# Norms: one over the root by token in columns, and eight layer norms with their means on TensorE

## The chip, the cores and the metric

The kernel runs on one core of a Trainium2 chip. The metric is the time of one execution on the device in microseconds (us). The engines: TensorE (PE; PEld is its weight load), VectorE (DVE), ScalarE (ACT), GpSimd (POOL) and SyncE (SP), which issues nearly all DMAs. Each engine works through its own instructions in the order in which they were placed, and waits for the others by semaphores.

## The reference

Two transformer blocks over 256 tokens with 1024 channels. The first has four branches (a softmax attention with forget gates, a recurrent unit, a stick-breaking attention, an attention to a memory), each gated, and a feed-forward part. The second has two layers over two streams (context and latent), each with a mixer (attention, gated linear attention, a convolution of width 31) and a feed-forward part. What this change touches are the norms:

```python
def _rms(x, g):
    y = x32 * lax.rsqrt(jnp.mean(x32 * x32, axis=-1, keepdims=True) + EPS)
    return y * g

def _layernorm(x, g=None, b=None):
    xc = xf - jnp.mean(xf, -1, keepdims=True)
    y = xc * lax.rsqrt(jnp.mean(xc * xc, -1, keepdims=True) + NORM_EPS)
    ...

def _modulate(x, shift, scale):
    return _layernorm(x) * (1.0 + scale) + shift

def _post(x, f, gate, g, b):
    return _layernorm(ALPHA * x + gate * f, g, b)
```

Every norm is over channels, so one number per token (or per token and head): the heads' norms of q and k in three attentions, of the linear attention's output, and the layer norms before and after each part.

## The kernel before

Activations lie with channels on the partitions: a stream is `[128, 8, 256]`, eight tiles of 128 channels by 256 tokens. Weights stream from HBM in units of 128x1024 (L438 to 470): a raw unit is split by ScalarE into a high part (`whi`) and by VectorE or GpSimd into a low part (`wlo`), and each product is three passes of 256 columns in a faster format (`mm<-hh,whi`, `hl,whi`, `hh,wlo`). In layer 1 some units go in plain fp32 (`mm<-h,raw`).

A sum over channels is a sum over partitions, and TensorE makes it: a product of a matrix of ones with the squares (L576 to 594, L807, L898, L1115, L1262) leaves the sum of each token in all 128 partitions, as 256 or 512 columns in the one PSUM buffer `st`. One over the root follows on VectorE in eight instructions (`rsqrt`, L530: a scale, a first guess from the bits, twice three instructions of Newton's step; tiles `nv`, `nr`, `nt`) over the same 256 or 512 columns. Its result multiplies the tiles directly, since it is in every partition.

Only two users have the sums in another shape: `token_rsqrt` (L542) lets the squares be the stationary operand and one column of ones the moving one, so the sums come out with tokens on the partitions, two or four columns in all, and the eight instructions are over 2 or 4 columns. The attentions that scale their logits by row use it.

A layer norm (`ln_core`, L603) has two forms. In the slow form VectorE adds the eight tiles (`fsum`, one reduction of 2048 elements), TensorE sums over partitions, VectorE centres all 2048 columns at once, ScalarE squares, VectorE adds the squares (`sq`), one product sums them, and `rsqrt` follows. In the fast form TensorE sums the eight tiles (eight products of 256 columns), VectorE centres two tiles at a time, TensorE sums the eight squares, ScalarE takes a square root and VectorE its reciprocal (`root`, L557). Thirteen of sixteen calls are slow.

A scheduler places the instructions by its own costs. Norms are written as generators that are interleaved with other parts (`weave`, `step`), so most norms have products of another part between their steps on TensorE.

Of the kernel before, what the change touches and what calls it, by code (L numbers as in the profile page):

```python
# [18 lines left out]
P = 128  # L19
D = 1024  # L20
T = 256
KT = 8
# [250 lines left out]
def run(*gens):  # L273
    for g in gens:
        for _ in g:
            pass
# [45 lines left out]
class Builder:  # L322
# [219 lines left out]
    def token_rsqrt(self, sq, nd, n):  # L542
# [9 lines left out]
        return self.rsqrt(ps[:, :2 * nh], 2 * nh, n)  # L552

# [22 lines left out]
    def total_sq(self, x, fast):  # L576
        ps = self.st()[:, :T]
        sq = []
        for f in range(0, KT, 2):
            a = self.t("sq", 512)  # L580
            self.act(a, flat(x[:, f:f + 2]), AF.Square)
            if fast:
                for j in range(2):
                    self.mm(ps, self.ones(), a[:, j * T:(j + 1) * T], start=f + j == 0, stop=f + j == KT - 1)
            else:
                sq.append(a)
                if f % 4:
                    self.tt(sq[-2], sq[-2], a, ALU.add)
# [5 lines left out]
        return ps  # L594

    def rms_h(self, x, g, hh, hl, fast=False):
        r = self.root(self.total_sq(x, fast), T, D)
# [5 lines left out]
    def ln_core(self, x, xc, fast=False):  # L603
# [6 lines left out]
        if fast:  # L610
            return self.root(self.total_sq(xc, True), T, D)
        return self.rsqrt(self.total_sq(xc, False), T, D)
# [55 lines left out]
    def block1(self, xt, ct, fill):  # L668
        nc = self.nc
        with self.pool("b1") as bp, self.phase("b1t", t1=4, t2=6):  # L670
# [7 lines left out]
            nc.sync.dma_start(self.pv[:, :late], self.a["pv"][:, :late])  # L678
            mh = newy()
# [52 lines left out]
            self.rms_h(xt, "ffn_g", *h, True)  # L732
# [74 lines left out]
    def mem_norm(self, ps, out, g):  # L807
# [4 lines left out]
        st = self.st()  # L812
        for j in range(2):
            self.mm(st[:, :T], self.ones(), sq[:, j * T:(j + 1) * T], start=j == 0, stop=j == 1)
        r = self.rsqrt(st[:, :T], T, 256)
# [60 lines left out]
    def fox(self, h, y, bp):  # L876
# [21 lines left out]
        def norm(ps, tag, g):  # L898
# [4 lines left out]
            self.mm(st, self.cst("b64"), sq)  # L903
            r = self.rsqrt(st, 512, 64)
# [210 lines left out]
    def qk_norm(self, ps, out, g):  # L1115
# [4 lines left out]
        st = self.st()  # L1120
        self.mm(st, self.ones(), sq)
        self.stt(out, raw, g, self.rsqrt(st, 512, 128), ALU.mult, ALU.mult)
# [72 lines left out]
    def gla_pair(self, l, hp, qk, vg, glr, S, new_S):  # L1195
# [50 lines left out]
        st = self.st()  # L1246
        for i in range(2):
# [14 lines left out]
            for dv in range(2):  # L1262
# [375 lines left out]
```

## Time and profile before

| | us |
|---|---|
| runs of the kernel | 3063.51 median (3053.55, 3063.51, 3064.5) |
| profiled execution, its own time | 3057.49 |
| its span in the profile | 3055.3 |
| PE busy | 2805.1 (92%) |
| DVE busy | 2004.4 (66%) |
| ACT busy | 1408.2 (46%) |
| POOL busy | 923.8 (30%) |
| granted PE clock, mean | 0.971 |

The span is cut into the parts of the program in order: block 1 with its four branches to about 850 us (its forget-gate attention from 240 to 430), the mixer of the context from 850 to 1400, that of the latent stream to 1850, two feed-forward parts to 2260, the memory and the mixer of layer 1 to 2845, a last feed-forward part. A row of a view gives busy time and the idle time in front of the instructions with what ended it; idle time of PE is the one that matters most, as it is the busiest engine.

### The profile page before, as it was taken

The page shows a single profiled execution, that of the slowest core. Times are in us where ns is not written, and L with a number is a line of the kernel's source. Part 1 is how long each engine was busy: PE and PEld are TensorE (multiplying, and loading weights), DVE is VectorE, ACT ScalarE, POOL GpSimd, SP SyncE. Part 2 cuts the span into 40 slices and gives each one's busy share as a digit, 9 for nine tenths or more (in the row PEclk, how much of TensorE's full clock was granted, in tenths as well). Part 3 has the DMA queues.
Part 4 walks back from the last instruction along what each step waited for, and adds up shares of the span by engine and source line. Part 5 has one row for each costly group of instructions (what it writes and reads, how often), then busy time and mean ns, then how long its engine had stood idle before and what let it go on. Part 6 is the DMA issues. An engine that isn't in the chain of part 4 may idle for free.

```text
span 3055.3 us, 51829 instructions
## 1 busy us (share of the span) xinstructions
PE 2805.1 (92%) x20816; PEld 2626.8 (86%) x20816; DVE 2004.4 (66%) x3305; ACT 1408.2 (46%) x2127; POOL 923.8 (30%) x684
## 2 busy tenths in 40 slices
PE   7998889999998878799999999999999999998898
PEld 6897778888898778788899988998898788898898
DVE  7597763347855999956798344467344499674554
ACT  5464456544445434345645554445434332354443
POOL 3243322233324444641102104444320113453000
PEclk9999999999999989899999999999999999999999
DMA  5443334566456554688567986654643223344353
GB/s 196 146 159 130 125 112 177 179 250 246 154 203 237 193 211 173 238 304 287 210 233 249 330 307 254 239 188 172 250 147 119 97 97 124 118 161 144 126 180 109
DMA packets 153425, 578.32 MB, mean 189 GB/s; under 512 B 17628, under 2 KB 17756, under 8 KB 146656
## 3 DMA queue, kind: packets, MB, share of 16 engines
q1 hardware_dynamic: 152496, 574.45, 53.2%
q8 instruction: 163, 2.67, 0.3%
q14 instruction: 78, 0.64, 0.1%
q10 hardware_dynamic: 688, 0.56, 0.1%
HBM read 516.73 MB, written 58.20 MB: 188 GB/s over the span
## 4 chain that ended last, share of the span: by engine, by line
PE 46%; DVE 19%; ACT 4%; DMA 2%; issue 1%; POOL 1%; SPq 0%; DVEq 0%; ACTq 0%; POOLq 0%
PE mm L371 38%; DVE ca L364 7%; PE st L371 2%; DVE gF L361 2%; DMA raw<-in_ws 2%; PE av L371 1%; DVE sq L361 1%; PE ga L371 1%; DVE wlo L361 1%; PE ad L371 1%; POOL wlo L361 1%; DVE fsum L572 1%; ACT whi L358 1%; PE ov L371 1%; PE lg L371 1%
## 5 line engine op out<-in xcount | busy, mean ns | idle before, releaser
L358 ACT ACTIVATE whi<-raw 128x1024 fp32r<-128x1024 f32 (+1 forms) x706 | 735.9, 1045 | 838.5 <-PE mm L371 529.3
L361 POOL TENSOR_TENSOR wlo<-raw,whi 128x1024 fp32r<-128x1024 f32 (+1 forms) x282 | 717.1, 2545 | 1046.1 <-ACT whi L358 825.6
L361 DVE TENSOR_TENSOR wlo<-raw,whi 128x1024 fp32r<-128x1024 f32 (+1 forms) x315 | 397.7, 1263 | 356.9 <-ACT whi L358 345.8
L371 PE MATMUL mm<-hh,whi 128*128 128x256 f32 x3376 | 504.6, 291 | 18.9 <-ACT hh L358 5.5
L371 PE MATMUL mm<-hh,wlo 128*128 128x256 f32 x3376 | 495.7, 288 | 15.2 <-DVE wlo L361 10.1
L371 PE MATMUL mm<-hl,whi 128*128 128x256 f32 x3376 | 493.0, 288 | 0.0
L371 PEld LDWEIGHTS mm<-hh,whi 128*128 128x128 f32 x3376 | 448.9, 196 | 43.7 <-issue 9.0
L371 PEld LDWEIGHTS mm<-hh,wlo 128*128 128x128 f32 x3376 | 448.4, 196 | 18.5 <-DVE wlo L361 10.5
L371 PEld LDWEIGHTS mm<-hl,whi 128*128 128x128 f32 x3376 | 446.9, 195 | 3.8 <-issue 3.1
L364 DVE SCALAR_TENSOR_TENSOR ca<-yp,pv,ca 128x256 f32<-128x256 f32 x720 | 360.9, 556 | 2.0
L371 PE MATMUL mm<-yh,whi 128*128 128x256 f32 x1152 | 174.6, 291 | 14.6 <-ACT yh L358 10.1
L371 PE MATMUL mm<-h,raw 128*128 128x256 f32 x800 | 181.9, 381 | 0.0
L361 POOL TENSOR_TENSOR gF<-cum 128x128 f32<-128x128 f32 x192 | 99.8, 550 | 255.0 <-PE ga L371 142.0
L371 PEld LDWEIGHTS mm<-yh,whi 128*128 128x128 f32 x1152 | 154.6, 195 | 21.2 <-ACT yh L358 13.2
L371 PE MATMUL mm<-yh,wlo 128*128 128x256 f32 x1152 | 168.1, 288 | 4.9 <-DVE wlo L361 3.9
L371 PE MATMUL mm<-yl,whi 128*128 128x256 f32 x1152 | 168.7, 288 | 2.6 <-DVE yl L364 2.6
L371 PEld LDWEIGHTS mm<-h,raw 128*128 128x128 f32 x800 | 150.3, 191 | 19.3
L371 PEld LDWEIGHTS mm<-yh,wlo 128*128 128x128 f32 x1152 | 152.4, 196 | 6.8 <-DVE wlo L361 4.1
L371 PEld LDWEIGHTS mm<-yl,whi 128*128 128x128 f32 x1152 | 152.9, 195 | 3.3 <-DVE yl L364 2.8
L371 PE MATMUL mm<-hidh,whi 128*128 128x256 f32 x704 | 102.9, 287 | 0.5 <-ACT hidh L358 0.5
L371 PE MATMUL mm<-hidl,whi 128*128 128x256 f32 x704 | 102.2, 286 | 0.0
L371 PE MATMUL mm<-hidh,wlo 128*128 128x256 f32 x704 | 101.5, 285 | 0.0
(280 smaller groups left out, 3840.6 us busy)
## 6 DMA issues: line engine op xcount, KB each, us to landing
raw<-in_ws SPq DMA_DIRECT2D x744, 512.0 KB, 3.8
lo<-wlo SPq DMA_DIRECT2D x109, 512.0 KB, 3.0
wlo<-lo SPq DMA_DIRECT2D x109, 512.0 KB, 4.2
wada<-in_wa SPq DMA_DIRECT2D x48, 1024.0 KB, 5.9
raw<-in_ws SPq DMA_DIRECT2D x32, 384.0 KB, 3.0
memt<-in_tok SPq DMA_DIRECT2D x4, 256.0 KB, 4.7
xt<-in_tok SPq DMA_DIRECT2D x1, 1024.0 KB, 7.1
ct<-in_tok SPq DMA_DIRECT2D x1, 1024.0 KB
```

The costliest lines, as they stand in the source:

```text
L358: return self.nc.scalar.activation(out, in_, f, **k)
L361: return (eng or self.nc.vector).tensor_tensor(out=out, in0=a, in1=b, op=op)
L364: return self.nc.vector.scalar_tensor_tensor(out=out, in0=a, scalar=s, in1=b, op0=op0, op1=op1)
L371: return self.nc.tensor.matmul(out, lhsT=l, rhs=r, start=start, stop=stop, **k)
L572: self.nc.vector.tensor_reduce(out=s, in_=x.rearrange("p f n -> p n f"), axis=AX.X, op=ALU.add)
```

## The change

`rsqrt` always works on columns with tokens on the partitions. A new helper, `spread`, brings the result back to all partitions: for each 128 tokens a product of the column, broadcast to 128 (or twice 64) columns as the stationary operand, with the identity; ScalarE copies the PSUM result to a tile. The norms of heads in the memory, the forget-gate attention, the keys and the linear attention, and all layer norms, sum by `token_rsqrt`-like products (128x128 stationary squares, one or two moving columns) and go through `spread`. The three RMS norms over all channels sum eight squares on TensorE and keep `root`. Eight calls of `ln_core` go from the slow to the fast form: the convolution's in three mixers, the latent and the context stream's norm after the mixer of layer 0, and three norms of the latent stream between the layers. The constants with the identity are loaded earlier.

```diff
     def rsqrt(self, ps, w, n):
-        new = self.col if w <= 4 else self.t
-        v, r, t = new("nv", w), new("nr", w), new("nt", w)
+        v, r, t = self.col("nv", w), self.col("nr", w), self.col("nt", w)
...
+    def spread(self, r, w, halves=False):
+        ps = self.st()
+        for i in range(w // P):
+            n = 2 if halves else 1
+            for c in range(n):
+                p = slice(c * P // n, (c + 1) * P // n)
+                self.mm(ps[p, i * P:(i + 1) * P], r[:, n * i + c:n * i + c + 1].to_broadcast([P, P // n]),
+                        self.cst("ident"))
+        out = self.t("nr", w)
+        self.act(out, ps[:, :w])
+        return out
...
+    def token_sq(self, x, fast):
+        ps = self.st()
+        sq = []
+        for f in range(0, KT, 2):
+            a = self.t("sq", 512)
+            self.act(a, flat(x[:, f:f + 2]), AF.Square)
+            sq.append(a)
+            if not fast and f % 4:
+                self.tt(sq[-2], sq[-2], a, ALU.add)
         if not fast:
-            a, b = sq[0], sq[2]
-            self.tt(a, a, b, ALU.add)
-            self.tt(a[:, :T], a[:, :T], a[:, T:], ALU.add)
-            self.mm(ps, self.ones(), a[:, :T])
+            a = sq[0]
+            self.tt(a, a, sq[2], ALU.add)
+            sq = [a]
+        n = 2 * len(sq)
+        for i in range(n):
+            for qt in range(2):
+                o = i % 2 * T + qt * P
+                self.mm(ps[:, qt:qt + 1], sq[i // 2][:, o:o + P], self.ones_t[:, :1], start=i + qt == 0,
+                        stop=i == n - 1, skip_group_check=True)
+        return ps[:, :2]
...
-        if fast:
-            return self.root(self.total_sq(xc, True), T, D)
-        return self.rsqrt(self.total_sq(xc, False), T, D)
+        return self.spread(self.rsqrt(self.token_sq(xc, fast), 2, D), T)
...
+            nc.sync.dma_start(self.cc, self.a["cst"])
...
             st = self.st()
-            self.mm(st, self.cst("b64"), sq)
-            r = self.rsqrt(st, 512, 64)
+            for i in range(4):
+                self.mm(st[:, 2 * i:2 * i + 2], sq[:, i * P:(i + 1) * P], self.cst("b64")[:, 0::64])
+            r = self.spread(self.rsqrt(st[:, :8], 8, 64), 512, True)
...
-        st = self.st()
-        self.mm(st, self.ones(), sq)
-        self.stt(out, raw, g, self.rsqrt(st, 512, 128), ALU.mult, ALU.mult)
+        r = self.spread(self.token_rsqrt([sq[:, :T], sq[:, T:]], 1, 128), 512)
+        self.stt(out, raw, g, r, ALU.mult, ALU.mult)
...
-        r = self.rsqrt(st, 512, 256).rearrange("p (h n) -> p h n", h=2)
+        r = self.spread(self.token_rsqrt(sqs, 2, 256), 512).rearrange("p (h n) -> p h n", h=2)
...
-        r = self.ln_core(ca, ca)
+        r = self.ln_core(ca, ca, True)
...
-        run(self.post(x, f"l1g{l}", f"l1b{l}", l == 1))
+        run(self.post(x, f"l1g{l}", f"l1b{l}", True))
```

Counted in the two programs, TensorE loses 63 products with ones of 256 columns and 12 of 512, and gains 64 of 256 columns (the fast form's means and the RMS norms), 308 with a moving operand of one or two columns, 80 of `spread` with 128 columns of output by 128 and 64 with 64 by 128. VectorE loses 35 chains of eight wide instructions, eight of thirteen reductions, 45 of the 60 additions of squares and three of six reciprocals; it gains 38 chains over 2 to 8 columns. ScalarE gains 38 copies of 256 or 512 columns.

The first place is the norm of the convolution's output in the context's mixer (`ca` is that output, `hh`, `hl`, `yh`, `yl` the operands of the gated products between). TensorE before:

```order
L371 MATMUL mm<-hl,whi 128x256 x8
L371 MATMUL mm<-hh,wlo 128x256 x5
L371 MATMUL st<-fsum,ones 128x256
L371 MATMUL mm<-hh,wlo 128x256 x3
L371 MATMUL mm<-yh,whi 128x256 x8
L371 MATMUL mm<-yl,whi 128x256 x8
L371 MATMUL mm<-yh,wlo 128x256 x8
L371 MATMUL mm<-hh,whi 128x256 x8
L371 MATMUL mm<-hl,whi 128x256 x8
L371 MATMUL mm<-hh,wlo 128x256 x8
L371 MATMUL mm<-yh,whi 128x256 x8
L371 MATMUL mm<-yl,whi 128x256 x3
```

TensorE at the same place now:

```order
L371 MATMUL st<-ca,ones 128x256 x8
L371 MATMUL mm<-hh,whi 128x256 x8
L371 MATMUL mm<-hl,whi 128x256 x8
L371 MATMUL mm<-hh,wlo 128x256 x8
L371 MATMUL st<-ones,sq 128x1 x8
L371 MATMUL mm<-yh,whi 128x256 x6
L371 MATMUL st<-ones,sq 128x1 x4
L371 MATMUL mm<-yh,whi 128x256 x2
L371 MATMUL mm<-yl,whi 128x256 x2
L371 MATMUL st<-ones,sq 128x1 x4
L371 MATMUL mm<-yl,whi 128x256 x6
L371 MATMUL mm<-yh,wlo 128x256 x7
```

Eight means and sixteen one-column sums stand where two products with ones stood; right behind the last row come the two products of `spread`, so 13 products stand between the last sum and them.

VectorE at this place before:

```order
L572 TENSOR_REDUCE fsum<-ca 128x256
L364 SCALAR_TENSOR_TENSOR gt<-gt,mm 128x256
L361 TENSOR_TENSOR acc<-acc,gt 128x256
L364 SCALAR_TENSOR_TENSOR ca<-st,ca 128x2048
L361 TENSOR_TENSOR wlo<-raw,whi 128x1024
L361 TENSOR_TENSOR sq<-sq 128x512 x3
L361 TENSOR_TENSOR sq<-sq 128x256
L368 TENSOR_SCALAR nv<-st 128x256
L368 TENSOR_SCALAR nr<-nv 128x256
L361 TENSOR_TENSOR nt<-nr 128x256
```

VectorE now:

```order
L364 SCALAR_TENSOR_TENSOR ca<-st,ca 128x512 x4
L368 TENSOR_SCALAR nv<-st 128x2
L368 TENSOR_SCALAR nr<-nv 128x2
L361 TENSOR_TENSOR nt<-nr 128x2
L364 SCALAR_TENSOR_TENSOR nt<-nt,nv 128x2
L364 SCALAR_TENSOR_TENSOR nr<-nt,nr 128x2
L361 TENSOR_TENSOR nt<-nr 128x2
L364 SCALAR_TENSOR_TENSOR nt<-nt,nv 128x2
L364 SCALAR_TENSOR_TENSOR nr<-nt,nr 128x2
L361 TENSOR_TENSOR wlo<-raw,whi 128x1024
```

The reduction and the additions of squares are gone, and the chain is over two columns.

The second place is the first key norm of the forget-gate attention (`kz` keys, `qz` queries, `lg` their logits), on TensorE. Before, from the sums of the squares on; 18 further rows, all `mm`, stand between the last row and the first logit:

```order
L371 MATMUL mm<-wlo,hh 128x256 x2
L371 MATMUL st<-hsq,cb 128x512
L371 MATMUL mm<-wlo,hh 128x256 x2
L371 MATMUL mm<-whi,hh 128x256 x4
L371 MATMUL mm<-whi,hl 128x256 x4
```

Now, up to the first logit but for ten rows of `mm` behind the last one here:

```order
L371 MATMUL mm<-wlo,hh 128x256 x2
L371 MATMUL st<-cb,hsq 128x2 x4
L371 MATMUL mm<-wlo,hh 128x256 x2
L371 MATMUL mm<-whi,hh 128x256 x4
L371 MATMUL mm<-whi,hl 128x256 x4
L371 MATMUL mm<-wlo,hh 128x256 x3
L371 MATMUL st<-cc,nr 64x128 x8
```

The sums are four narrow products, 13 products later stand the eight of `spread`, and the first logit comes after 50 products of 256 columns instead of 90.

## Rows read from the trace of the kernel before

**Rows 1.** The page: the span and part 1, busy time by engine.
```profile
span 3055.3 us, 51829 instructions
PE 2805.1 (92%) x20816; PEld 2626.8 (86%) x20816; DVE 2004.4 (66%) x3305; ACT 1408.2 (46%) x2127; POOL 923.8 (30%) x684
```
**Rows 2.** By stretch: length, PE, PEld, DVE, ACT, POOL busy (instructions), clock, DMA.
```profile
240.00:430.00 190.00, 161.53 (x1165) 145.98 (x1164) 137.19 (x220) 82.42 (x148) 59.74 (x30) 0.96 0.35 119
990.00:1290.00 300.00, 238.34 (x1700) 228.92 (x1698) 287.77 (x472) 117.66 (x164) 152.80 (x126) 0.90 0.57 204
1560.00:1700.00 140.00, 136.06 (x1042) 131.81 (x1042) 113.07 (x257) 69.06 (x88) 29.94 (x45) 0.99 0.75 262
1700.00:1850.00 150.00, 136.66 (x1078) 132.42 (x1078) 79.93 (x133) 76.68 (x118) 15.12 (x9) 0.99 0.84 306
2000.00:2110.00 110.00, 102.04 (x804) 100.10 (x803) 86.83 (x104) 53.95 (x80) 44.47 (x20) 0.95 0.48 169
2260.00:2310.00 50.00, 47.03 (x229) 40.60 (x228) 38.27 (x62) 25.25 (x45) 2.06 (x18) 1.00 0.31 111
2460.00:2630.00 170.00, 155.51 (x827) 136.85 (x827) 168.69 (x377) 49.56 (x73) 46.16 (x54) 0.97 0.31 108
```
**Rows 3.** The chain that ended last from 1085 to 1300, by line.
```profile
by line: PE mm L371 25.0%; DVE ca L364 25.0%; issue 6.4%; DVE gF L361 5.7%; POOL wlo L361 5.6%; PE ov L371 4.5%; DVE wlo L361 3.8%; PE ga L371 3.2%; PE st L371 2.8%; DVE sq L361 1.8%; PE gs L371 1.7%; DVE fsum L572 1.7%; ACT gF L358 1.3%; D
```
**Rows 4.** Groups by line and form on DVE: count, busy, mean ns, idle before.
```profile
L364 DVE SCALAR_TENSOR_TENSOR nr<-nt,nr 128x512 f32<-128x512 f32 x36 | 37.7, 1047 | 0.6
L364 DVE SCALAR_TENSOR_TENSOR nt<-nt,nv 128x512 f32<-128x512 f32 x36 | 35.3, 980 | 0.7
...
L361 DVE TENSOR_TENSOR nt<-nr 128x512 f32<-128x512 f32 x36 | 29.1, 808 | 1.0
...
L368 DVE TENSOR_SCALAR nv<-st 128x512 f32<-128x512 f32 x18 | 12.4, 688 | 25.5 <-PE st L371 25.4
L368 DVE TENSOR_SCALAR nr<-nv 128x512 int32<-128x512 int32 x18 | 12.2, 677 | 0.3
...
L361 DVE TENSOR_TENSOR nt<-nr 128x2 f32<-128x2 f32 x8 | 1.3, 158 | 0.2
L368 DVE TENSOR_SCALAR nr<-nv 128x2 int32<-128x2 int32 x4 | 0.7, 169 | 0.1
```
**Rows 5.** Groups by line and form on PE, with what ended the idle time.
```profile
L371 PE MATMUL st<-sq,ones 128*128 128x256 f32 x94 | 29.1, 448 | 35.6 <-DVE sq L361 27.3 <-ACT sq L358 8.0
...
L371 PE MATMUL st<-fsum,ones 128*128 128x256 f32 x26 | 9.7, 458 | 14.3 <-DVE fsum L572 14.3
L371 PE MATMUL lg<-kz,qz 128*128 128x128 f32 x32 | 7.0, 303 | 17.7 <-DMA kz<-ncf 14.0 <-DVE wlo L361 3.7
```
**Rows 6.** Timeline at a narrow norm of the memory attention: start, length, instruction, count.
```profile
86.54 0.97 PEld L371 LDWEIGHTS st<-ones,hsq 128*128 128x128 f32 x8 [0.21 <-ACT hsq L358]
...
87.43 0.30 PEld L371 LDWEIGHTS mm<-hh,whi 128*128 128x128 f32 x2
...
87.64 0.16 DVE L368 TENSOR_SCALAR nv<-st 128x2 f32<-128x2 f32 x1 [0.37 <-PE st L371]
...
88.42 0.16 DVE L364 SCALAR_TENSOR_TENSOR nr<-nt,nr 128x2 f32<-128x2 f32 x1
```
**Rows 7.** Timeline of weight loads at products of 128 columns.
```profile
1627.71 0.97 PEld L371 LDWEIGHTS ga<-gF 128*128 128x128 f32 x8 [0.82 <-issue]
1628.60 0.42 PEld L371 LDWEIGHTS mm<-hh,whi 128*128 128x128 f32 x3
```
**Rows 8.** Timeline at a fast layer norm: its means and its centring.
```profile
2806.02 3.33 PEld L371 LDWEIGHTS st<-xt,ones 128*128 128x128 f32 x16
...
2809.79 2.48 DVE L364 SCALAR_TENSOR_TENSOR xt<-st,xt 128x512 f32<-128x512 f32 x4 [1.45 <-PE st L371]
```
**Rows 9.** Timeline: a narrow norm's instruction beside one of GpSimd.
```profile
1035.67 2.38 POOL L361 TENSOR_TENSOR wlo<-raw,whi 128x1024 fp32r<-128x1024 f32 x1 [4.22 <-ACT whi L358]
...
1035.70 2.37 DVE L361 TENSOR_TENSOR nt<-nr 128x4 f32<-128x4 f32 x1
```

More of the change, by code (lines that the diff above doesn't have):

```diff
@@ L574, in total, with total_sq @@
         return ps
-    def total_sq(self, x, fast):
+    def total_sq(self, x):
         ps = self.st()[:, :T]
+        for f in range(0, KT, 2):
+            a = self.t("sq", 512)
+            self.act(a, flat(x[:, f:f + 2]), AF.Square)
+            for j in range(2):
+                self.mm(ps, self.ones(), a[:, j * T:(j + 1) * T], start=f + j == 0, stop=f + j == KT - 1)
+        return ps
+    def token_sq(self, x, fast):
+        ps = self.st()
         sq = []
@@ L581, in total_sq, with rms_h @@
             self.act(a, flat(x[:, f:f + 2]), AF.Square)
-            if fast:
[L583 to L588, printed above, removed]
-        if not fast:
-            a, b = sq[0], sq[2]
-            self.tt(a, a, b, ALU.add)
-            self.tt(a[:, :T], a[:, :T], a[:, T:], ALU.add)
-            self.mm(ps, self.ones(), a[:, :T])
-        return ps
-    def rms_h(self, x, g, hh, hl, fast=False):
-        r = self.root(self.total_sq(x, fast), T, D)
+            sq.append(a)
+            if not fast and f % 4:
+                self.tt(sq[-2], sq[-2], a, ALU.add)
+        if not fast:
+            a = sq[0]
[8 more added lines that the diff above has]
+        return ps[:, :2]
+    def rms_h(self, x, g, hh, hl):
+        r = self.root(self.total_sq(x), T, D)
         for f in range(KT):
@@ L811, in mem_norm @@
         self.act(sq, ps, AF.Square)
-        st = self.st()
-        for j in range(2):
-            self.mm(st[:, :T], self.ones(), sq[:, j * T:(j + 1) * T], start=j == 0, stop=j == 1)
-        r = self.rsqrt(st[:, :T], T, 256)
+        r = self.spread(self.token_rsqrt([sq[:, :T], sq[:, T:]], 2, 256), T)
         for j in range(2):
@@ L1261, in gla_pair @@
             self.act(qkp[:, i].rearrange("p d n -> p (d n)"), ov)
-            for dv in range(2):
-                self.mm(st[:, i * T:(i + 1) * T], self.ones(), sq[:, dv * T:(dv + 1) * T], start=dv == 0,
-                        stop=dv == 1)
-        r = self.rsqrt(st, 512, 256).rearrange("p (h n) -> p h n", h=2)
+            sqs += [sq[:, :T], sq[:, T:]]
+        r = self.spread(self.token_rsqrt(sqs, 2, 256), 512).rearrange("p (h n) -> p h n", h=2)
         for dv in range(2):
@@ L1602, in program @@
             with b.pool("m1") as bp, b.phase("m1t", t1=4, t2=6, t4=4):
-                run(b.post(xt, "l2g0", "l2b0"))
-                h = b.modulated(xt, ax1, 0, h2, native="both")
+                run(b.post(xt, "l2g0", "l2b0", True))
+                h = b.modulated(xt, ax1, 0, h2, True, "both")
                 b.native = True
```

9 lines of the change are left out of this document (3 added, 6 removed).

## The prediction

> **What bounds the kernel now.** I read the page's engine shares first. TensorE is busy for 2805 of 3055 us, VectorE for 2004, the other two for less than half [rows 1]. So work added to TensorE is paid unless it falls into one of its 250 idle us, and work taken from VectorE is worth what TensorE waits for it. The table by stretch says where that is. From 990 to 1290 us, in the context's mixer, VectorE is busy 288 of 300 us and TensorE idle for 62, at a mean clock of 0.90 [rows 2]. The chain of waits agrees: from 1085 to 1300 it lies as much on the convolution's instructions on VectorE (`ca`, 25.0%) as on the weight products (25.0%), with 1.7% on the reduction `fsum` and 1.8% on the sums of squares [rows 3]. From 2460 to 2630 VectorE is as full (169 of 170 us), but TensorE idles 14 us only. In the forget-gate attention, 240 to 430, TensorE idles for 28 us. From 1700 to 1850 the DMA engines carry most (0.84). Elsewhere TensorE is full: from 2260 to 2310, two layer norms one behind the other, it idles 3 us [rows 2].
>
> The groups by form then say what the norms cost. A chain over 512 columns takes 0.69 + 0.68 + 2 x (0.81 + 0.98 + 1.05) = 7.0 us on VectorE on the mean, 18 of them; over two columns it is eight instructions of 0.16, 1.3 us [rows 4]. TensorE's waits for norms are the sums of squares (27.3 us for VectorE, some of it at the start), the reductions (14.3) and the logits of the forget-gate attention, which wait for the normed keys and the DMA behind them (17.7) [rows 5].
>
> **What TensorE gains in work.** A product of ones with 256 columns is 3.33 us for eight, 0.42 each [rows 8]; 512 columns I take as two, 0.84. A sum with one moving column isn't free: four of them hold the weight loads from 86.54 to 87.43, 0.22 each [rows 6]. Products of 128 columns cost the same, 0.89 us for four [rows 7]. The trace has no product with a broadcast stationary operand; I bound it by nothing and by twice that row and take the row, 0.22. For those with 64 columns in two halves I take half, 0.11, between 0 and 0.22. Added: 64 x 0.42 = 26.9, 308 x 0.222 = 68.4, 80 x 0.222 = 17.8, 64 x 0.11 = 7.0, in all 120. Removed: 63 x 0.42 = 26.5 and 12 x 0.84 = 10.1, in all 37. Net +83.5 us, of which each layer norm that goes to the fast form has 3.4 + 3.6 + 0.4 - 0.8 = 6.5, eight of them 52; the eight head norms of the forget gates have 7.4, the six of the linear attention 5.9.
>
> Not all of this is paid. In the stretch at 990, where VectorE sets the pace, two linear-attention norms (2.0) and the convolution's norm (6.5) fall into idle time: -8.5. From 1700 to 1850, with DMA at 0.84, two norms (13) do so by half: -6.5. If these covers fail the whole is paid. To pay: **+68.5**.
>
> **The new wait.** Today no product waits for a norm's chain directly, except through tiles that VectorE multiplies later. Now TensorE has the product of `spread` in its own queue, and behind it all weight products. Mostly 13 products stand between the last sum and `spread`. By three loads in 0.42 us [rows 7] these take 1.6 to 1.8 us. The chain needs 0.21 us until VectorE starts and 8 steps of 0.195 (four steps from 87.64 to 88.42), 1.8 us [rows 6]. Where VectorE is free the wait is thus 0 to 0.2 us; other work in VectorE's queue adds some. 38 x 0.26: **+10**, between 0 and 84: a narrow instruction beside one of GpSimd took 2.37 us instead of 0.16, until that one ended [rows 9, 4]; 38 x 2.2 is the upper end.
>
> The Trainium skill's page "Advanced Engine Details and Errata", section "GPSIMD Details", says that GpSimd shares a read and a write interface with VectorE and conflicts with instructions of two SBUF inputs; six of the eight in a chain are such, however narrow. The trace agrees (2.37 us beside 2.38). By this rule, with GpSimd busy 30% of the time, an estimate is 38 x 0.3 x 1.2 = 14 us on top of the 10; by the row of the undisturbed chain, nothing. It speaks against the change, as such a stall now stops TensorE; it stands behind the slower rival below.
>
> **What goes.** In the forget-gate attention the chain over 512 columns becomes 1.3 us, twice per pair of heads. With 50 products instead of 90 between key sums and logits there is less in front of them, some 7 us, and the new path (chain 1.8, `spread` and copy about 1.7, the multiplication, the DMA) needs about as much. I take 16 of the 17.7 us, and 6 of the 190 x 0.04 = 7.6 that the clock loses there [rows 5, 2]: **-22**, bounds -5 and -28.
>
> At 990 to 1290 VectorE's queue sets the end, so what leaves it counts: two chains of 7.0 down to 1.3, -11.5; the reduction and the squares' additions of the convolution's norm, 3.5% of 215 us on the chain [rows 3], 7.5, and 1 for the rest of its chain: **-20**, bounds -8 and -35.
>
> The other seven norms that become fast: from 2000 to 2110 there are three slow norms, and TensorE loses 8.0 us idle and 110 x 0.05 = 5.5 by its clock, 4.5 each; in 2260 to 2310 two norms lose 3.0, 1.5 each [rows 2]. Five at the first rate and two at the second: **-25**, bounds -5 and -32. After the eight means 24 products stand in front of the squares' sums, 2.9 to 3.4 us, and the centring of four pieces takes 2.5 [rows 8]; so little new waiting follows.
>
> The last four norms of the linear attention take 4 x 5.7 = 23 us off VectorE in two stretches where TensorE is nearly full too; a third: **-8**, bounds 0 and -23. VectorE's load falls by a good 5% by the 512-wide chains alone (127 to 23 us [rows 4]). Of the 150 us or so of idle TensorE that I have not named, 7% go: **-10**, bounds 0 and -30.
>
> ScalarE's 38 copies lie beside its idle half; if one is late the multiplication behind it is. The five norms that stay slow and the three that were fast change by less than 1 us each and are in the count of products. The constants' load now stands ahead of the first weights on SP's queue; the eight RMS products run while the tiles arrive. I take the start at 0, within 2 us.
>
> Sum: 68.5 + 10 - 22 - 20 - 25 - 8 - 10 = -6.5. The profiled execution took 3057.5 us in all, 2.2 more than its span, and the median of the runs 3063.5. So 3051 in terms of the former, **3057** as a median. About 0.5%, 15 us, is what a measurement of this kernel can tell from no change.
>
> **The rivals.** *A, the forecast*: added products and removed waits cancel, 3035 to 3077. Chance 0.50.
>
> *B, VectorE's relief reaches further.* For it: the stretch at 990 has 62 us of idle TensorE and a clock of 0.90, and GpSimd holds wide instructions up, so shorter norms free the weights' low parts as well. Against it: outside of it TensorE is hardly idle. Conv stretch -35 instead of -20, the linear attention -18, the rest -25, little new waiting (+3): 47 less, 3010. Chance 0.20.
>
> *C, TensorE now stands behind VectorE and GpSimd, slower.* The place is `spread` behind its chain, above all where GpSimd splits weights or the convolution fills VectorE's queue. Price: 38 x 1.5 = 57 instead of 10, 3104. It decides (3079 and more) from a mean wait of (10 + 22) / 38 = 0.84 us. For it is the 2.37 us row, against it that most chains have no other instruction in between in the new order. Here the columns also wouldn't be as short as said. Chance 0.18.
>
> *D, the norms' waits were hidden anyway.* With other products interleaved the fast norms' waits come back at other places: -5 instead of -25, forget gates -10 instead of -22. That is 32 more, 3089. For it is 2260 to 2310, where two norms cost 3 us; against it the clock at 2000. Chance 0.12.
>
> Below 3048 lie 0.18 of A and 0.20 of B: faster 0.38. Above 3079 lie 0.02 of A, 0.16 of C and 0.10 of D: slower 0.28. The rest, 0.34, is no change. B's 3010 is the lower end; of C I leave out the part above 3095: 3010 to 3095, with A's own 3035 to 3077.
>
> **What would show it.** TensorE's busy time up by some 70 to 90 us at a similar span, VectorE's down by 150 or more. `st<-ones,sq` at 0.22 us per product. Idle time in front of `st<-cc,nr` of about 10 us in all (C: over 30). The wait of `lg<-kz` under 3 us instead of 17.7. From 990 on, the convolution's end 15 to 20 us earlier; from 2260 to 2310 the two norms about 10 us later at their end. The forecast is wrong if the narrow sums run at another price than 0.22, if the idle time before `spread` is several times that, or if the stretch at 990 doesn't shorten.

## The result, and the profile after

The changed kernel takes 3105.31 us (median; 3099.49 to 3112.19), the kernel before on the same chip 3059.61 (3053.55 to 3064.5): a ratio of 1.0140, 95% interval 1.0122 to 1.0158. It is 43 us slower (a ratio step of 0.001 is 3.06 us). That lies outside the predicted range of 3010 to 3095, and it is the sign that the forecast held for the least likely of the three. The profiled execution took 3104.2 us, its span 3102.4.

The page, span and part 1, as [rows 1] for before:

```profile
span 3102.4 us, 53661 instructions
PE 2901.6 (94%) x21698; PEld 2732.8 (88%) x21698; DVE 1814.7 (58%) x3291; ACT 1424.2 (46%) x2159; POOL 917.2 (30%) x690
```

TensorE is busy for 96.5 us more, VectorE for 189.7 less. The span grew by 47.1, so TensorE's idle time fell by 49 only. The forecast had counted on 83.5 us of work and 85 of waits and low clock that go. The stretches below hold about the same work as those of [rows 2], at about their new places (stretch and length, busy us of PE, PEld, DVE, ACT, POOL, then the granted clock as a share of 2.4 GHz, the DMA share and GB/s):

```profile
248.00:430.00 182.00, 169.39 (x1332) 155.01 (x1331) 94.08 (x228) 88.35 (x163) 54.83 (x29) 0.97 0.37 122
994.00:1295.00 301.00, 245.95 (x1767) 236.94 (x1766) 268.05 (x481) 119.33 (x169) 150.66 (x125) 0.90 0.58 204
1715.00:1871.00 156.00, 153.28 (x1192) 149.75 (x1192) 58.05 (x126) 77.94 (x121) 18.16 (x12) 0.96 0.80 294
2021.00:2132.00 111.00, 105.59 (x831) 103.63 (x830) 72.44 (x100) 54.19 (x83) 41.16 (x20) 0.95 0.47 159
2282.00:2340.00 58.00, 58.00 (x315) 51.26 (x313) 22.33 (x57) 27.48 (x47) 3.51 (x20) 0.97 0.28 96
```

Windows cut at round times miss some products, so from here on places are compared by progress: the time by which as many of the products that two kernels have in common (the sums and spreads left out) are done, at a time given in the kernel before. The changed kernel lies 7.9 us behind the kernel before at 240 us and 2.7 at 482, so the forget-gate attention is 5 us shorter. It lies 3.9 behind at 990 and 4.1 at 1350: the context's mixer, which was to lose 20, loses nothing, although VectorE does 20 us less there. It lies 23.7 behind at 2260 and 36.5 at 2325, so the two norms between cost 13. And in two of the stretches with flipped norms (norms that went from the slow to the fast form) the clock is lower than before: 0.96 for 0.99 at 1700, 0.97 for 1.00 at 2260.

The groups by form on TensorE (count, busy us and mean ns of one, idle before and what ended it) answer to [rows 5]; a product in fp32 has two records, so 392 are 196 products:

```profile
L371 PE MATMUL st<-ones,sq 128*128 128x1 f32 x392 | 53.5, 264 | 9.0 <-ACT sq L358 8.3 <-DVE ca L364 0.7
L371 PE MATMUL st<-cc,nr 128*128 128x128 f32 x160 | 28.4, 317 | 16.0 <-DVE nr L364 15.5
L371 PE MATMUL st<-cc,nr 128*64 128x128 f32 x128 | 9.3, 289 | 1.2 <-DVE nr L364 0.6
L371 PE MATMUL lg<-kz,qz 128*128 128x128 f32 x32 | 6.2, 275 | 0.0
L371 PE MATMUL st<-fsum,ones 128*128 128x256 f32 x10 | 4.3, 518 | 3.8 <-DVE fsum L585 3.8
```

The waits that were to go did go: 17.7 us before the logits to 0, 27.3 for VectorE's sums of squares to 0.7, 14.3 for the reductions to 3.8. The new wait before the spread is 17.2 us for 38 norms, 0.45 each. The narrow sums take 53.5 / 196 = 0.27 us each in this view. That isn't to be held against the forecast's 0.22, which is read from the starts of weight loads: in this view the kernel before has 16.6 / 64 = 0.26.

```profile
L371 PE MATMUL st<-ones,hsq 128*128 128x1 f32 x128 | 16.6, 251 | 0.9 <-ACT hsq L358 0.8
```

So the mean price is about as it was, and what goes wrong shows only in order of time. Windows around the narrow run of one layer norm:

```profile
1843.00:1847.50 4.50, 4.50 (x32) 4.27 (x32) 2.48 (x4) 1.81 (x3) 2.21 (x1) 1.00 0.72 227
1847.50:1851.00 3.50, 3.50 (x34) 3.50 (x32) 1.23 (x1) 1.51 (x3) 0.00 (x0) 1.00 0.30 95
1851.00:1853.00 2.00, 2.00 (x14) 2.00 (x15) 0.04 (x1) 0.00 (x0) 0.00 (x0) 0.72 0.47 184
1853.00:1858.00 5.00, 5.00 (x24) 5.00 (x25) 2.19 (x9) 1.44 (x2) 0.00 (x0) 0.50 0.00 0
1858.00:1862.00 4.00, 4.00 (x33) 4.00 (x32) 3.05 (x7) 3.20 (x8) 1.51 (x2) 0.91 0.67 242
```

and the timeline of TensorE there (start, length, instruction and count of a group):

```profile
1846.67 1.12 PE L371 MATMUL mm<-hh,wlo 128*128 128x256 f32 x8
1847.63 1.88 PE L371 MATMUL st<-ones,sq 128*128 128x1 f32 x16
...
1850.16 0.95 PE L371 MATMUL st<-ones,sq 128*128 128x1 f32 x8
...
1851.53 1.40 PE L371 MATMUL st<-ones,sq 128*128 128x1 f32 x8
...
1854.21 1.70 PE L371 MATMUL mm<-hh,wlo 128*128 128x256 f32 x7
1855.71 1.05 PE L371 MATMUL st<-cc,nr 128*128 128x128 f32 x4
```

TensorE is busy in every one of these windows to the last hundredth, no DMA or engine holds it up, and yet its granted clock falls from 1.00 (2.4 GHz) to 0.50 (1.2 GHz) in the course of the narrow run. Eight records take 0.95 us at 1850.16 and 1.40 at 1851.53; seven weight products at 1854.21 take 1.70, where eight took 1.12 at 1846.67. There are eleven such runs of 16 products. In the trace they take 4.1 to 6.3 us each, 56.5 together with the weight products that stand inside some of them (the sums alone 48.4), where the forecast had 11 x 3.55 = 39. The clock falls within four of them (1282, 1732, 1848 and 2033 us) with at most 0.7 us of idle time in the 10 us in front. In four others (1407, 2294, 2309 and 2744) it holds to the run's end, and falls right behind two of these. The last three (2857, 2874 and 3085) stand behind 2.7 us of idle time or more, so their low clock isn't the sums' alone.

### The profile page after: what moved, and what is told of

It is laid out like the page before. It is cut to its first block, busy times and chain, and to the rows that moved or that the text cites. A ratio compares the mean times of both kernels' runs of the same rounds, so it can differ in the third digit from the quotient of the medians.

```text
span 3102.4 us, 53661 instructions
## 1 busy us (share of the span) xinstructions
PE 2901.6 (94%) x21698; PEld 2732.8 (88%) x21698; DVE 1814.7 (58%) x3291; ACT 1424.2 (46%) x2159; POOL 917.2 (30%) x690
## 4 chain that ended last, share of the span: by engine, by line
PE 71%; DVE 18%; ACT 4%; issue 3%; DMA 2%; POOL 1%; SPq 0%; ACTq 0%; DVEq 0%; POOLq 0%
PE mm L371 56%; PE st L371 5%; DVE ca L364 5%; DVE gF L361 2%; PE av L371 2%; DVE wlo L361 2%; PE ad L371 2%; ACT whi L358 2%; DMA raw<-in_ws 1%; PE lg L371 1%; PE ga L371 1%; PE ov L371 1%; POOL wlo L361 1%; DVE ht L364 1%; PE z L371 1%
## 5 line engine op out<-in xcount | busy, mean ns | idle before, releaser
L361 POOL TENSOR_TENSOR wlo<-raw,whi 128x1024 fp32r<-128x1024 f32 (+1 forms) x282 | 701.3, 2489 | 1048.9 <-ACT whi L358 841.3
L361 DVE TENSOR_TENSOR wlo<-raw,whi 128x1024 fp32r<-128x1024 f32 (+1 forms) x315 | 406.1, 1290 | 437.3 <-ACT whi L358 398.6
L371 PE MATMUL mm<-hh,wlo 128*128 128x256 f32 x3376 | 493.1, 288 | 13.9 <-DVE wlo L361 10.0
L371 PEld LDWEIGHTS mm<-hh,wlo 128*128 128x128 f32 x3376 | 446.6, 195 | 16.6 <-DVE wlo L361 10.4
L371 PE MATMUL mm<-yh,whi 128*128 128x256 f32 x1152 | 178.2, 294 | 14.6 <-ACT yh L358 10.6
```

What stands on the lines that cost most here:

```text
L361: return (eng or self.nc.vector).tensor_tensor(out=out, in0=a, in1=b, op=op)
L371: return self.nc.tensor.matmul(out, lhsT=l, rhs=r, start=start, stop=stop, **k)
```

## The experiments

Theory 1 is that the added products are paid nearly in full where TensorE is full. Theory 3 says why VectorE's relief brought nothing from 990 to 1290, theory 4 that the narrow runs cost clock. Rivals are C (the wait before the spread), D (waits come back elsewhere), and the forecast's own steps. Ratios are to the kernel before, run on the same chip.

**The forget gates alone**, in the kernel before:

```diff
-            self.mm(st, self.cst("b64"), sq)
-            r = self.rsqrt(st, 512, 64)
+            for i in range(4):
+                self.mm(st[:, 2 * i:2 * i + 2], sq[:, i * P:(i + 1) * P], self.cst("b64")[:, 0::64])
+            r = self.spread(self.rsqrt(st[:, :8], 8, 64), 512, True)
```

> The kernel before, with nothing changed but the eight head norms of the forget-gate attention: narrow sums, columns, the product that spreads them. Theory 1 (added products are paid wherever TensorE is full, and the waits that go are worth only what its idle time there shrinks): as in the changed kernel, where the stretch from 244 to 452 us became 8.8 us shorter, so 9 us faster than before, 3051, a ratio of 0.997. The step of the forecast (22 removed, 7.4 added): 15 us faster, 0.995. Rival D (the waits come back elsewhere, 10 removed): 3 us faster, 0.999.

Measured 3051.51, ratio 0.9965 (0.9954 to 0.9976), 10.7 us faster. Theory 1 is nearest. The stretch of [rows 2] in this kernel (windows), and its logits (groups):

```profile
240.00:430.00 190.00, 178.81 (x1421) 163.16 (x1421) 97.55 (x241) 93.02 (x173) 56.77 (x30) 0.99 0.36 123
```

```profile
L371 PE MATMUL lg<-kz,qz 128*128 128x128 f32 x32 | 6.4, 284 | 1.8 <-DMA kz<-ncf 1.8
```

Idle time falls from 28.5 to 11.2 us and the clock is 0.99 instead of 0.96, as forecast. By progress this kernel lies 1.8 us behind the kernel before at 240 and 7.2 ahead at 482, so the stretch gives 9 where the forecast has 14.6, and most of it stays (9.5 ahead at 1230). Single instructions mislead here, as the two kernels interleave them otherwise: at 428 us the attention's own products lie 15 us earlier, the weight products between them 4 to 6.

**The linear attention as well** (`gla_pair` as in the change, on top of the forget gates):

```diff
-        r = self.rsqrt(st, 512, 256).rearrange("p (h n) -> p h n", h=2)
+        r = self.spread(self.token_rsqrt(sqs, 2, 256), 512).rearrange("p (h n) -> p h n", h=2)
```

> The kernel before with the forget gates' head norms and the linear attention's six in columns; layer norms, memory and keys as before. Theory 1: 10.7 from the forget gates as measured alone, and for the linear attention 6.6 us as the kernel with slow layer norms gained at 1215 to 1237, less some 4 of added products in the stretches where TensorE is full: 3050 for 3063, a ratio of 0.996. The forecast's steps (12 of the 20 at 990 and 8 later, less 5.9 of work): 14 us on top of the forget gates', 3040.

Measured 3053.32, ratio 0.9966 (0.9950 to 0.9983): the six norms bring nothing by time, where the forecast had 15.6; the two ratios leave room for some 6 us. In the traces, this kernel wins 5.7 us on the kernel before from 990 to 1350 and the one with the forget gates alone 2.2, so some 3.5 of the forecast's 11.5 there are seen.

**Layer norms back in the slow form**, the rest as changed (five places, one shown):

```diff
-        r = self.ln_core(ca, ca, True)
+        r = self.ln_core(ca, ca)
```

> The changed kernel with the eight layer norms back in the slow form, means and sums of squares on VectorE, the rest as changed. Theory 1: the stretches with these norms became 24 us longer (9.2 from 1616 to 1793, 0.5 from 1793 to 2090, 14.6 from 2090 to 2336, 0 at the convolution's norm), so 24 us less than the changed kernel, some 3081; TensorE's busy time falls by about 52. Rival (the flips are worth what they cost, and it is the head norms' products and the wait before the spread that cost): within 5 us of the changed kernel, 3100 to 3110. The forecast's own terms (52 paid in work, 8 to 15 hidden, 25 won): 14 less, 3091.

Measured 3068.58, ratio 1.0024 (1.0014 to 1.0034): 36 us less than the changed kernel, more than theory 1 had from the stretches, and TensorE is busy for 2850.3 us, 51 less. So most of the loss comes with the flips as they are made here: they add 51 us on TensorE and bring back 15.

**A constant column into the spread**, so that no product waits for a chain (it leaves out the scale of the norms):

```diff
-                self.mm(ps[p, i * P:(i + 1) * P], r[:, n * i + c:n * i + c + 1].to_broadcast([P, P // n]),
+                self.mm(ps[p, i * P:(i + 1) * P], self.flat_t[:, n * i + c:n * i + c + 1].to_broadcast([P, P // n]),
```

> The changed kernel with the spread's product reading a constant column (0.1) instead of the norm's result: the same products and the same chains on VectorE, but TensorE never waits for them. It leaves out the scale of the norms. Theory 1: no more than the idle time seen in front of the spread goes, 17 us (and 10 if the time comes back at the next wait), so 3088 to 3095. Rival C (TensorE stands behind VectorE and GpSimd at the spread and this is what makes the change slow): 40 us or more, 3065 or less.

Measured 3092.98, ratio 1.0094 (1.0077 to 1.0111), 14 us less than the changed kernel. The wait before these products is gone:

```profile
L373 PE MATMUL st<-cc,flat 128*128 128x128 f32 x160 | 29.3, 326 | 1.4 <-DVE nv L370 1.4
```

The mean granted clock of this execution is lower (0.961 for 0.966, some 15 us), for a reason that stays open; so the wait may be worth more than 14, up to some 29. The 40 us that C asked for are not there, and C falls.

**The first two RMS norms as before:**

```diff
-        r = self.root(self.total_sq(x), T, D)
+        r = self.root(self.total_sq(x, fast), T, D)
```

> The changed kernel with the first two RMS norms as before: VectorE adds the squares, one product sums them. Theory 1 with its start: in the changed kernel the eight products of the first norm run while the tiles arrive, then TensorE idles and its clock is at 0.77 and 0.54 from 10 to 30 us (1.00 before); the first 106 us became 7.9 longer. If the early products bring the low clock, 6 to 8 us less than the changed kernel, 3098, and a clock of 1.00 from 10 to 30 us. Rival (the start is longer for the memory's head norms and their spread): within 2 us of the changed kernel, and the low clock stays.

Measured 3103.86, ratio 1.0126 (1.0112 to 1.0141), some 4 us less, which the two intervals don't set apart. The clock from 10 to 30 us, of the changed kernel, then of this one from 0 to 30:

```profile
10.00:20.00 10.00, 2.86 (x9) 1.56 (x9) 9.01 (x17) 5.58 (x10) 5.02 (x3) 0.77 0.85 337
20.00:30.00 10.00, 9.50 (x47) 9.07 (x47) 3.67 (x6) 2.13 (x4) 5.03 (x4) 0.54 0.43 166
```

```profile
0.00:10.00 10.00, 0.00 (x0) 0.00 (x0) 2.29 (x6) 4.00 (x6) 1.10 (x12) 1.00 0.74 245
10.00:20.00 10.00, 3.21 (x8) 2.00 (x8) 8.85 (x15) 4.52 (x7) 4.69 (x2) 1.00 0.88 354
20.00:30.00 10.00, 8.20 (x47) 7.91 (x48) 3.89 (x10) 4.69 (x9) 3.83 (x4) 1.00 0.40 158
```

Weight products in the timelines, of the changed kernel and then of this one, which also waits at the spread of the memory's norm:

```profile
25.75 1.91 PE L371 MATMUL mm<-yh,wlo 128*128 128x256 f32 x8
29.16 1.12 PE L371 MATMUL mm<-yl,whi 128*128 128x256 f32 x8
```

```profile
25.32 1.91 PE L371 MATMUL mm<-yl,whi 128*128 128x256 f32 x8
28.02 1.12 PE L371 MATMUL mm<-yh,whi 128*128 128x256 f32 x8
60.12 1.20 PE L371 MATMUL st<-cc,nr 128*128 128x128 f32 x4 [5.58 <-DVE nr L364]
```

The 1.00 of this kernel is no measured clock: the windows give 1.00 also from 0 to 10 us, where it has no product at all, and the trace has no record of its clock before 27 us. The products decide. Eight of them take 1.91 us at 25 us in both kernels and 1.12 from 28 or 29 us on, so TensorE is slow at first in both; in the kernel before, too, eight take 1.65 at 23.82 and 1.12 at 26.25. The expectation's "1.00 before" doesn't hold, and the early products don't bring the low clock. Both kernels lie 1.8 to 1.9 us behind the kernel before at 30 us, and 7.6 and 6.1 at 60: what makes the start longer comes behind 30 us. There the changed kernel has the eight products of the second norm (3.70 us at 36.51); without them the spread of the memory's norm waits 5.58 us for VectorE instead of 1.85. The rival is nearer. Seven other kernels with the changed kernel's start lie 4.5 to 7.4 us behind at 130 us, so the size varies with the execution.

**Two splits of GpSimd given to VectorE.** The trace of the changed kernel shows, where the first linear-attention norm was cut down, GpSimd and VectorE side by side:

```profile
1119.43 11.20 POOL L361 TENSOR_TENSOR wlo<-raw,whi 128x1024 fp32r<-128x1024 f32 x1 [4.84 <-ACT whi L358]
```

```profile
1118.44 9.98 DVE L364 SCALAR_TENSOR_TENSOR ca<-yp,pv,ca 128x256 f32<-128x256 f32 x25
1135.37 1.23 DVE L361 TENSOR_TENSOR wlo<-raw,whi 128x1024 fp32r<-128x1024 f32 x1 [6.94 <-ACT whi L358]
```

A split whose median is 2.40 us takes 11.20, and ends 2.2 us after VectorE's row of 25 convolution steps does. TensorE waits 3.99 us for it; VectorE, done early, then idles 6.94. In the kernel before the chain of 512 columns stood between the steps, and the split at this place took 4.19. But a long split isn't new (the kernel before has one of 8.24 us at 1221, beside 18 convolution steps; there the changed kernel has 4.46), and TensorE's two waits at this place, before and then now, are equally long:

```profile
1130.88 2.07 PE L371 MATMUL mm<-yh,wlo 128*128 128x256 f32 x8 [3.90 <-DVE wlo L361]
1144.14 0.69 PE L1289 MATMUL gt<-cc,gw 128*128 128x128 f32 x2 [8.50 <-DVE gw L361]
```

```profile
1130.68 1.32 PE L371 MATMUL mm<-hh,wlo 128*128 128x256 f32 x8 [3.99 <-POOL wlo L361]
1149.95 0.69 PE L1310 MATMUL gt<-cc,gw 128*128 128x128 f32 x2 [8.88 <-DVE gw L361]
```

So the held split adds no wait; it stands where the wait was to go. The edit:

```diff
-            self.split(raw[:, :n], hi[:, :n], lo[:, :n])
+            self.split(raw[:, :n], hi[:, :n], lo[:, :n], self.pick(self.lo_eng()))
+def pick(self, eng):
+    self.n_pool = getattr(self, "n_pool", 0) + (eng is self.nc.gpsimd)
+    return self.nc.vector if self.n_pool in (138, 139) else eng
```

> The changed kernel with two weight splits of the context's mixer, those that GpSimd makes from 1119 to 1133 us (11.20 and 2.37 us), given to VectorE; nothing else. Theory 3 (the chains taken from VectorE brought nothing from 990 to 1290 because VectorE's convolution steps close up behind each other, 25 in a row, and hold up GpSimd's split, for which TensorE then waits): the wait of 3.99 us at 1130 goes, the carry product that waits for the decay tile (8.88 us, at 1150) comes 4 to 7 us earlier, and some of that stays, 3098 to 3102 for 3105. The forecast's step (VectorE's work in all sets the end of the stretch, and 2.4 us are added to it): 0 to 3 us slower.

Measured 3104.57, ratio 1.0137 (1.0120 to 1.0154), no difference by time. In the trace theory 3's step is there: no wait for a split is left at that place, VectorE does both in 2.35 us, and the same instructions lie 9.8 us earlier than in the changed kernel at 1192 and 5.6 earlier at 1303. But by progress this execution lay 4.3 us earlier at 1100 already, in front of the two splits, so only some 5.5 of the 9.8 and 1.3 of the 5.6 are the edit's. Later the difference fades: 9 earlier at 1861, 8 at 2566, 1 at 2860.

```profile
1117.67 2.35 DVE L361 TENSOR_TENSOR wlo<-raw,whi 128x1024 fp32r<-128x1024 f32 x2
```

**Less work on VectorE at 990**, in the kernel before (it leaves out the last seven steps of the context's convolution):

```diff
-        conv = self.conv(l, yps, ca)
+        conv = self.conv(l, yps, ca, 31 if mem else 24)
```

> The kernel before with 24 of the 31 steps of the context's convolution (it leaves out the last seven of each of the eight tiles): 56 instructions of 0.41 us on VectorE, 23 us, nothing else. The forecast's step (from 990 to 1290 VectorE's queue sets the end, so what leaves it counts in full): 17 to 23 us faster, 3041 to 3047. Theory 3 (the end hangs on single waits, for splits and decay tiles, with slack on VectorE between them): under 10 us, 3054 or more.

Measured 3049.55, ratio 0.9959 (0.9947 to 0.9972): 12.6 us for 23 taken away. Neither end holds; a bit over half of what leaves VectorE counts, and the split waits again in its place:

```profile
1129.71 2.08 PE L371 MATMUL mm<-yh,wlo 128*128 128x256 f32 x8 [4.90 <-POOL wlo L361]
1146.70 0.69 PE L1289 MATMUL gt<-cc,gw 128*128 128x128 f32 x2 [7.86 <-DVE gw L361]
```

**The narrow sums twice**, into two columns nobody reads:

```diff
-                self.mm(ps[:, qt:qt + 1], sq[i // 2][:, o:o + P], self.ones_t[:, :1], start=i + qt == 0,
+                for q in range(2 if fast else 1):
+                    self.mm(ps[:, 2 * q + qt:2 * q + qt + 1], sq[i // 2][:, o:o + P], self.ones_t[:, :1],
+                            start=i + qt + q == 0, stop=i == n - 1, skip_group_check=True)
```

> The changed kernel with the narrow sums of the eleven fast layer norms issued twice, the second time into two other columns that nobody reads: 11 x 16 more products of 0.22 us, 39 us of TensorE. Theory 1 (paid in full where TensorE is full): 32 to 39 us slower than the changed kernel, 3137 to 3144. Rival (narrow products lie beside the wait for the centring and the squares that stands there anyway, as the forecast had for 15 of 68 us and rival D for more): 20 us or less, 3125.

Measured 3181.8, ratio 1.0392 (1.0375 to 1.0409): 77 us over the changed kernel for 39 us of work. No theory of that time allowed for it. The windows of one run of 32 products, from 1862.9 us on, gave theory 4:

```profile
1863.00:1865.50 2.50, 2.50 (x25) 2.50 (x24) 1.23 (x1) 1.38 (x3) 0.00 (x0) 1.00 0.53 185
1865.50:1867.00 1.50, 1.50 (x10) 1.50 (x9) 0.00 (x0) 0.00 (x0) 0.00 (x0) 0.56 0.83 259
1867.00:1870.00 3.00, 3.00 (x16) 3.00 (x15) 0.00 (x0) 0.00 (x0) 0.00 (x0) 0.50 0.11 45
```

25 records in 2.5 us, then 16 in 3.0: the rate nearly halves with the clock, with nothing else running at the end and no gap. In this kernel the clock is at half for a part of every one of the eleven runs, seven of them with no idle time of TensorE in the 10 us in front, and its mean over the execution is 0.954 for the changed kernel's 0.966.

**128 columns of ones instead of one**, same count:

```diff
-                self.mm(ps[:, qt:qt + 1], sq[i // 2][:, o:o + P], self.ones_t[:, :1], start=i + qt == 0,
-        return ps[:, :2]
+                self.mm(ps[:, qt * P:(qt + 1) * P], sq[i // 2][:, o:o + P], self.ones(), start=i + qt == 0,
+        return ps[:, 0:T:P]
```

> The changed kernel with one operand changed: the layer norms' sums take 128 columns of ones as the moving operand instead of one, and the chain reads one column of each 128. The same number of products, and by the rows of 128-column products (0.22 us each) the same time at the full clock. Theory 4 (in a run of narrow sums TensorE is busy without a gap, yet its granted clock falls from 1.00 to 0.50 some 3 us after the run's start and stays there until behind the spread; the changed kernel has eleven such runs, together 56.5 us instead of 39.3): the clock stays at 1.00, 17 us from the runs and 5 to 15 from the products behind them, 3073 to 3083. Rival (the clock falls there for another reason, as for the long run of fp32 weight loads, or these runs are hidden): within 5 us of the changed kernel, 3105, and the runs again 5 to 6 us.

Measured 3085.99, ratio 1.0067 (1.0052 to 1.0082), 22 us less than the changed kernel. Windows at the norm shown above, and its run in the timeline:

```profile
1842.00:1846.00 4.00, 4.00 (x38) 4.00 (x36) 1.38 (x2) 1.42 (x3) 0.00 (x0) 1.00 0.34 110
1846.00:1848.00 2.00, 1.82 (x17) 1.65 (x15) 1.14 (x8) 0.00 (x0) 0.00 (x0) 1.00 0.11 43
1848.00:1853.00 5.00, 5.00 (x44) 5.00 (x44) 4.16 (x7) 3.93 (x8) 1.63 (x2) 1.00 0.18 41
```

```profile
1842.03 3.77 PE L371 MATMUL st<-ones,sq 128*128 128x128 f32 x32
```

The clock stays at 1.00 through the run and behind it. Eight of the eleven runs take 3.73 to 3.81 us now; the last three, which follow idle time, 5.4, at a clock of 0.69 to 0.70. The mean clock of the execution is 0.972 for 0.966, some 19 us, while the sums themselves take 51.9 us for 53.5: what is won is clock. Theory 4 holds, at the low end of its gain; in the two profiled executions the gain is 13.9 us. One thing more differs: the run stands in one piece, where the changed kernel has weight products inside most of its runs. That it is the one column and not this mixture is not shown apart.

**The same, twice:**

```diff
+                for q in range(2 if fast else 1):
+                    self.mm(ps[:, (2 * q + qt) * P:(2 * q + qt + 1) * P], sq[i // 2][:, o:o + P], self.ones(),
```

> The kernel whose layer norms sum with 128 columns of ones, with these products issued twice in the eleven fast norms, the second time into other columns that nobody reads: 176 more of 0.22 to 0.24 us, 39 to 42 us of TensorE. Theories 1 and 4 (products at the full clock, paid in full): 35 to 42 us over 3086, 3121 to 3128; the 76 that the one-column products cost when they were doubled were 39 of work and the rest clock. Rival (doubling costs twice its work for another reason, as by waits behind longer runs): 60 us or more over 3086.

Measured 3125.13, ratio 1.0202 (1.0180 to 1.0223): 41 us over the former. The group, 51.9 us for 392 records there:

```profile
L371 PE MATMUL st<-ones,sq 128*128 128x128 f32 x744 | 91.0, 285 | 9.2 <-ACT sq L358 8.0 <-DVE ca L364 1.2
```

39.1 us more work, 41 us more time, at the same mean clock (0.972): at the full clock the products are paid in full, as theory 1 says. So of the 77 us of the one-column doubling about half was clock.

**The fast norms with wide sums and the root:**

```diff
+        if fast:
+            return self.root(self.total_sq(xc), T, D)
```

> The changed kernel with the fast layer norms in the form that three of them had before: eight products of ones with the squares, 256 columns, ScalarE's square root and VectorE's reciprocal over 256 columns, no spread; the slow norms and the heads stay in columns. Theory 4 (the narrow runs cost clock): 11 x 0.64 us less of work, 7 us, and 20 to 30 of clock and of the wait for the spread, 3070 to 3080, if the square root brings no wait of its own. Theory 1 alone (work by its count at 0.22): 7 us and the waits of eleven spreads, 5, so 3093. Rival (the flips are what costs, whichever the sums): 3100 or more.

Measured 3076.84, ratio 1.0041 (1.0029 to 1.0053), 30 us less than the changed kernel and 5 more than with slow norms. The mean clock is 0.975. Theories 1 and 4 together.

**A version that beats both**: the forget gates and the linear attention in columns, and the two splits on VectorE (the edits above, in the kernel before).

> The kernel before with the forget gates' and the linear attention's norms in columns, and the two weight splits that GpSimd holds for 11.19 and 2.37 us at 1111 to 1125 given to VectorE. Theory 3: what the two splits gave in the changed kernel up to 1303 us (5.6 us) is kept, since no long narrow run follows: 3047 to 3050 for 3064 (0.995 to 0.996; without the splits 0.9966). Rival (the convolution's end hangs on VectorE's sum, to which 2.4 us are added): no gain over 0.9966, 3053 or more.

Measured 3047.88, ratio 0.9948 (0.9931 to 0.9965). It is faster than both kernels. Against the one without the splits (0.9966) the intervals overlap; in the traces the same instructions lie 5.5 us earlier at 1303, but 2.2 of it stood at 1100 already, in front of the splits. So the splits give some 3 us of the stretch of [rows 3] in this pair of traces, which the times don't tell apart.

## Why the prediction was wrong

The runs make a ladder from before to after, each step beside what the prediction's terms give for it (work at its prices, less what it hid or won; a measured step is a difference of two ratios, good to about 5 us):

| step | forecast, us | measured, us |
|---|---|---|
| forget gates in columns | 7.4 - 22 = -14.6 | -10.7 |
| linear attention in columns | 5.9 - 2 - 11.5 - 8 = -15.6 | +0.3 |
| memory, keys, RMS, all layer norms in columns, 13 of them slow | 25.4 - 10 = +15.4 | +17.8 |
| eight norms flipped, wide sums and root in all eleven | 38 - 13 - 8.5 - 25 = -8.5 | +5.2 |
| narrow sums of 128 columns and the spread in these | +7.0 | +8.0 |
| one column instead of 128 | 0 | +22.4 |
| the wait before the spread | +10 | in the steps above; 14 by the run without it |
| in all | -6.3 | +43.0 |

- **What bounds the kernel** was right: TensorE. 39 us of products at the full clock cost 41.
- **The price of a narrow sum is the step that failed most.** "A sum with one moving column isn't free: four of them hold the weight loads from 86.54 to 87.43, 0.22 each" [rows 6]. That row is of four products. The change issues sixteen, in one row or with a few weight products between, and in the course of such a run, in four of eleven, the clock goes to half, for the rest of the run, the spread and some products behind it. With 128 columns it doesn't: 22 us by experiment, of the 49 between forecast and result, and the forecast had not one for it. The row was read rightly; the term lacked the clock. The prediction named it among what would make it wrong ("if the narrow sums run at another price than 0.22"), yet no rival carried it.
- The Trainium skill's page "TensorE: Matmul & The Clock Gate", section "Part 1: The HAM clock gate", puts TensorE's low clock down to idle time. By that rule nothing would have been lost in the run shown above, in which TensorE is busy by the profile without a gap; the trace differs, and the measurement decides.
- **The stretch at 990 is the second failed step** ("VectorE's queue sets the end, so what leaves it counts"). Of its 20 us, 11.5 were the linear attention's: the run with these norms alone gives nothing by time, later ones included (8 forecast), and some 3.5 us in the trace. The run with fewer convolution steps shows that the premise is half true, 12.6 of 23. By progress the changed kernel lies 3.9 us behind at 990, 0.6 at 1230 and 4.1 at 1350, and with slow layer norms 1.2, -2.1 and -3.8: some 3 us were won up to 1230, and the convolution's norm, which was to win 8.5, costs some 5 against its slow form. Where the norm's chain had stood, VectorE's convolution steps close up, and GpSimd's split goes from 4.19 to 11.20 us beside them. The prediction had seen that pair in [rows 9], as a stall of VectorE by GpSimd, and put it behind rival C; it came the other way round. The Trainium skill's page "Advanced Engine Details and Errata", section "GPSIMD Details", which speaks of an interface that the two engines share, agrees with it in this direction too (11.20 us beside 9.98). How much of this stretch is lost this way stays open; by 1303, two splits gave 1.3 us back in the changed kernel and 3.3 in the other, by one trace each.
- **The flips.** With wide sums they cost 5 where the terms give -8.5; the convolution's norm, counted as hidden (-6.5) and winning 8.5, is the likely part: from 1230 to 1500, with its norm and the one behind it, the kernel with wide sums falls 6 us further behind the one with slow norms (the changed kernel 10). That is read from progress, not from a run of its own. Of the two behind 1793, the first cost the changed kernel nothing (17.7 us behind at 1800, 17.8 at 1870), the second 6 (23.7 at 2110).
- **The forget gates**: mechanism right, the size too large: 14.6 forecast, 10.7 by time and 9 in the stretch.
- **The new wait**: 17.2 us in the trace instead of 10, 14 by the run without it. Rival C's sign was right, its mechanism was not: a mean of 0.45 us lies far from the 0.84 from which it decides. Rival D has its part at 990, where the waits come back.
- **The start**, taken at 0 within 2 us, was 7.9 late in the profiled execution: 1.9 at 30 us and 7.6 at 60. The low clock from 10 to 30 us is not the cause, as the kernel before is slow there too.
- The "rest", 10 us won with VectorE's load, can't be told apart: the step that holds it measured 17.8 for 15.4, with 25.4 of work and the new waits in it.

## What to carry to other kernels

Price a new instruction by a row of a run as long as the one that is added, and look at the granted clock within it; four products in a row told nothing of sixteen. Before time taken off an engine is booked as a gain, ask which instruction closes up into the gap and whom that one holds up. And in this kernel, with TensorE busy for 92% of the time, taking VectorE's wide work over was a loss where the wait it removed was not larger than the products; for the forget gates alone it was. In a trace, compare places by progress and from before the edit on: single instructions, and two executions, differ by as much as what is looked for.

## What the runs showed of the hardware that was not expected

- TensorE's clock fell from 1.00 to 0.50 with the engine busy without a gap, in runs of fp32 products with one moving column (records of 0.112 us before, 0.213 after); with 128 moving columns the same products took 0.236 us each and the clock stayed at 1.00 in eight of the eleven runs (the other three follow idle time). Of the runs with one column, in four (1407, 2294, 2309 and 2744 us) it did not fall within the run; over the 12 us from their start it was 0.86, 1.00, 0.86 and 1.00. Why not there stays open.
- A subtraction on GpSimd, 2.40 us by the median, took 11.20 beside 25 back-to-back instructions of VectorE with two inputs in SBUF, and 11.19 at the same place in another kernel; the kernel before has one of 8.24 beside 18 such instructions.
- TensorE's first products ran slowly whether they began at 4.85 us or at 10.43: eight of 256 columns took 1.91 us at 25 us in either kernel, and 1.12 at 28 to 29.
